# A 64-row product in two PSUM banks in place of a zero-padded one, the output gate made one block later, and a seventh weight buffer

## The chip, the cores and the metric

The kernel runs on one core of a Trainium2 chip. The metric is the device time of one execution in microseconds. A core has a matrix engine (TensorE: PE in the profile, PEld its weight loads), VectorE (DVE), ScalarE (ACT), GpSimd (POOL) and a queue engine (SP) that here issues every DMA. SBUF is the on-chip memory of 128 partitions; PSUM, into which TensorE writes, has eight banks of 512 fp32 values per partition.

## What is computed

A decoder block over 2048 positions and 1024 channels, with two mixers side by side; cut from the reference:

```python
mod = jnp.einsum('bd,de->be', jax.nn.silu(c), ada_w[l]) + ada_b[l]
shift, scale, gate = jnp.split(mod, 3, axis=-1)
h = _rmsnorm(x, norm_g[l]) * (1.0 + scale[:, None, :]) + shift[:, None, :]
p = jnp.einsum('bsd,de->bse', h, w_in[l])            # 1024 -> 9344 channels
...
# RWKV-7 mixer, 16 heads of 64, for every position t:
sk = jnp.einsum('bhvk,bhk->bhv', state, kk_t)
state = (state * w_t[:, :, None, :] - sk[..., None] * b_t[:, :, None, :]
         + v_t[..., None] * k_t[:, :, None, :])
out_t = jnp.einsum('bhvk,bhk->bhv', state, r_t)
...
m = jax.nn.sigmoid(g_conv) * y_conv + jax.nn.sigmoid(g_rwkv) * y_rwkv
out = jnp.einsum('bsd,de->bse', m, w_out[l])
x = x + gate[:, None, :] * out
return _rmsnorm(x, final_g)
```

`y_conv` is a causal depthwise convolution of width 31 with a layer norm and gates. The gate of the last-but-one line is one number per channel, made from `c` alone; the kernel multiplies it into the columns of `w_out`.

## The kernel before

**Stages.** The sequence is cut into four blocks of 512 positions (`NB`, `TB`). The first stage (to about 2500 us) runs over the blocks, and in a block over four groups of four heads; the second stage does the output projections of all blocks. Each of the first three blocks also makes the input of the next one (`xnorm`), and the last one begins the second stage's work for block 0.

**Projections.** Every weight tile (128 channels, 1024 x 128, 4 KB per partition) is used as two parts, a rounded high part and the rest, and three products are summed (`mm3k`, L205). In block 0, `load_w` loads the fp32 tile (`w_st`, L185), ScalarE rounds it (L188), VectorE or GpSimd subtracts (L190), and both parts are stored to DRAM (L194, L195); the later blocks load the two parts (L181, L182). All of these share the pool tag "w" with `WB` = 6 buffers.

**A group.** `group` (L575) drives two pairs of heads through `pair` (L457), a generator in three steps, in the order `ORD`; then it inverts small triangular blocks on GpSimd (L627, L629), and runs the state over eight chunks of 64 positions (L677 to L701): a product of the state into an `xo` bank (L686), 64 x 64 products (L691), and the update of the state (L697, L701). A pair holds two heads of 64 channels: head 0 on partitions 0 to 63, head 1 on 64 to 127.

**The A products** (L528 to L541) are the third step of a pair: for each head and each chunk, a 128 x 128 matrix of products between the tiles `BK` and `KR` over the head's 64 channels. The eight chunks go in two quarters of four (`c4`). To keep one head out of the other's product, ScalarE copies the head's 64 rows of `BK` into `BKz` (L531), a tile of 4 KB per partition whose other 64 rows were set to zero once at the start (L287 to L289), and TensorE multiplies over all 128 rows (L537). Each head's four products fill one bank of tag "aux", and VectorE multiplies it with a mask into `As` (L539).

**PSUM.** Eight banks: two "main" for projections, one "late", `PXB` = 2 for "xo" (the scan), one for the convolution, and `PAB` = 2 for "aux", which the steps of `pair` and L599 use in turn. In block 0 the first four projections are made while the input comes in (`hprep0`, L379), and hold the two "main" and the two "xo" banks until they are used.

**The gate.** `silu_row` makes the row silu(c), broadcast over the partitions, in a buffer of tag "KR" (L260). After the first group of block 0 (`GG` = 0) `ada_cols` loads eight rows of the gate's matrix in pieces of 128 x 1024 into buffers of tag "As", multiplies and sums each on VectorE (L225), and the finished gate goes to DRAM as `grow_d` (L911 to L916).

**Stored weights.** The weights of the second stage are made in spare places: `ogate` (L147) loads a half tile of `w_out`, multiplies it with the gate from DRAM (L156), splits it (L157, L158) and stores both parts; `keep` (L164) does the same without a gate for the two other output projections (L170 to L173). Block 1 does the 16 halves of `ogate`, block 2 the 32 halves of `keep`. They use the shared tag "hx" of seven buffers of 2 KB (`HXB`), as do the input norm and others.

**The order of the work** on each engine is laid down when the program is built: the tile framework keeps the dependencies, and a simulated timeline with priorities decides which ready instruction comes next in an engine's queue. On the chip each queue runs in that order. The loops that fill a group with projections (`NEXT`, `FIRST`, `fill`) are written by hand.

Of the kernel before, what the change touches and what calls it, by code (L numbers as in the profile page):

```python
# [9 lines left out]
F32 = mybir.dt.float32  # L10
# [3 lines left out]
ALU = mybir.AluOpType  # L14
# [4 lines left out]
P = 128  # L19
D = 1024  # L20
KT = D // P
TB = 512
NTT = TB // P
CH = 64
NCH = TB // CH
# [6 lines left out]
KRB, TKB, ASB = 4, 3, 4  # L32
# [2 lines left out]
W2 = 4  # L35
HB = 8
HXB = 7
GG = 0
PXB, PAB = 2, 2
VVT, SHT, RKT, RHT, YT = "r", "sh", "k", "sh", "M"  # L40
ORD = (0, 0, 1, 0, 1, 1)
OE, LE, CE = 0, 0, 1
WLL = 1
TRE = 1
MS, MS2 = 2, 1
WB = 6
KEPT = ("in",)
def lplan(t):
    n = {"c": 0, "g": 0}
# [33 lines left out]
def hybrid_block(ctx: ExitStack, tc: tile.TileContext, x, vecs, convk, w2a2, final_g, ada, w_in, w_co, w_ro, w_o, crow, out,  # L83
                 seq=2048, groups=(0, 1, 2, 3), phase2=True, dbg=None):
    nc = tc.nc
# [4 lines left out]
    cst = ctx.enter_context(tc.tile_pool(name="cst", bufs=1))  # L90
    whl = ctx.enter_context(tc.tile_pool(name="whl", bufs=2))
    dp = ctx.enter_context(tc.tile_pool(name="dp", bufs=1, space=DRAM))
# [10 lines left out]
    u_dram = [dp.tile([P, TB], F32, name=f"u_d{j}", tag=f"u_d{j}") for j in range(KT)]  # L103

    grow_d = dp.tile([D], F32, name="grow_d", tag="grow_d")


    ident = cst.tile([P, P], F32, name="ident")
# [6 lines left out]

    g_col = cst.tile([P, KT], F32, name="g_col")
    hgate_col = cst.tile([P, KT], F32, name="hgate_col")
    shift_col = cst.tile([P, KT], F32, name="shift_col")
    ones = cst.tile([P, P], F32, name="ones")
    nc.vector.memset(ones, 1.0 / D)  # L120
# [11 lines left out]
    def flat(ap):  # L132
        return ap.rearrange("p a b -> p (a b)")
# [85 lines left out]
    def ada_cols(srow, pool, tag, bufs, pairs):  # L219

        for rows, dsts in pairs:
            st = pool.tile([P, 2, D], F32, name="ada_st", tag=tag, bufs=bufs)
            for m in range(2):
                nc.sync.dma_start(st[:, m, :], ada[rows[m]])
                nc.vector.scalar_tensor_tensor(out=st[:, m, :], in0=st[:, m, :], scalar=1.0, in1=srow, op0=ALU.mult,  # L225
                                               op1=ALU.mult, accum_out=dsts[m])
            yield
# [19 lines left out]
    pm = ctx.enter_context(tc.tile_pool(name="pm", bufs=2, space=PSUM))  # L247
    c1 = late.enter_context(tc.tile_pool(name="c1", bufs=1))
    l3 = late.enter_context(tc.tile_pool(name="l3", bufs=3))
# [15 lines left out]
    ab = vc("ada_b")  # L265
# [16 lines left out]
    def headsum(ps, full, hi):  # L282
# [1 line left out]
        nc.gpsimd.tensor_tensor(out=lo, in0=full, in1=hi.bitcast(F32), op=ALU.subtract)  # L284
        nc.tensor.matmul(ps, bones, hi, start=True, stop=False)
        nc.tensor.matmul(ps, bones, lo, start=False, stop=True)
    BKz = c1.tile([P, 2, NCH // 4, 4 * CH], F32, name="BKz")  # L287
    nc.gpsimd.memset(BKz[64:128, 0], 0.0)
    nc.gpsimd.memset(BKz[0:64, 1], 0.0)  # L289
    hones = bones.bitcast(F32)[:, 0::64]  # L290
    keepm = c1.tile([P, TB // 2], mybir.dt.bfloat16, name="keepm")
    nc.vector.memset(keepm, 1.0)
# [38 lines left out]
    def hx(name):  # L331
        return xp.tile([P, TB], F32, name=name, tag="hx")
# [44 lines left out]
    front = {}  # L377

    def hprep0(xs, ada_steps):  # L379


        ss = e2.tile([P, 5, NTT], F32, name="ss0", tag="ss0", bufs=1)
        s2, ss, rs, rt = ss[:, 0:2, :], ss[:, 2, :], ss[:, 3, :], ss[:, 4, :]
        for tt in range(NTT):
            for half in range(2):
                nc.scalar.activation(hx("xsq0"), xs[tt][:, half * TB:half * TB + TB], AF.Square,
                                     accum_out=s2[:, half, tt:tt + 1])
        nc.vector.tensor_tensor(out=ss, in0=s2[:, 0, :], in1=s2[:, 1, :], op=ALU.add)
        nc.vector.tensor_scalar(out=ss, in0=ss, scalar1=1.0 / D, scalar2=RMS_EPS, op0=ALU.mult, op1=ALU.add)
        rsqrt(rs, ss, None, nc.vector, rt)  # L390
        dg = e2.tile([P, NTT, P], F32, name="dg", tag="yj", bufs=1)
        for tt in range(NTT):
            nc.vector.tensor_scalar(out=dg[:, tt, :], in0=ident, scalar1=rs[:, tt:tt + 1], scalar2=None, op0=ALU.mult)
        h = ([], [])
        tiles_ = (T_LORA, T_K, T_R, T_V)
        wf_ = {}
        for k in range(KT):
            next(ada_steps)
            pt = (pl, pc)[k % 2].tile([P, NTT, P], F32, name="ps_x", tag=("late", "acc")[k % 2])
            for tt in range(NTT):  # L400
                nc.tensor.matmul(pt[:, tt, :], xs[tt][:, k * P:(k + 1) * P], dg[:, tt, :], start=(tt == 0),
                                 stop=(tt == NTT - 1), skip_group_check=True)
            hf = hx("hf0")
            nc.scalar.activation(hf, flat(pt), AF.Identity, scale=g_col[:, k:k + 1], bias=shift_col[:, k:k + 1])
            hsplit(h, k, hf)
            for i, ti in enumerate(tiles_):
                if k == i // 2:
                    hl = None
                    if i >= 2:
                        hl = [l3.tile([P, KT, P], F32R, name="w_f", tag="tk", bufs=TKB) for _ in range(4 - i)]  # L410
                        if i == 3:
                            hl.append(lt.tile([P, KT, P], F32R, name="w_f", tag="La", bufs=1))
                    wf_[ti] = load_w("in", ti, hl)
                    front[ti] = (pm, px)[i // 2].tile([P, TB], F32, name="ps_f", tag=("main", "xo")[i // 2])

            for i, ti in enumerate(tiles_):
                if ti in wf_ and k > i // 2:
                    for kk in range(0 if k == i // 2 + 1 else k - 1, k):
                        mm3k(front[ti], wf_[ti], h, kk)
        for ti in tiles_:  # L420
            mm3k(front[ti], wf_[ti], h, KT - 1)
        return h
# [34 lines left out]
    def pair(b, q_, pr, h, lora, uv, Asb, rn, res):  # L457
# [68 lines left out]
        yield  # L526

        for c4 in range(NCH // 4):  # L528
            for hh in range(2):
                hs = slice(64 * hh, 64 * hh + 64)  # L530
                nc.scalar.copy(BKz[hs, hh], BK[hs, c4 * 2:c4 * 2 + 2])  # L531
            for hh in range(2):
                pA = pa.tile([P, 2, 256], F32, name="aux", tag="aux")
                for c in range(4):
                    cc, e = (c4 * 4 + c) // 2, c % 2
                    es = slice(e * 128, e * 128 + 128)
                    nc.tensor.matmul(pA[:, c // 2, es], BKz[:, hh, c // 2, es], KR[:, cc, es],  # L537
                                     start=(c == 0), stop=(c == 3), skip_group_check=True)
                nc.vector.tensor_tensor(  # L539
                    out=Asb[:, hh, c4 * 4:c4 * 4 + 4, :].rearrange("p (a e) n -> p a (e n)", e=2),  # L540
                    in0=pA, in1=flat(maskA).unsqueeze(1).broadcast_to([P, 2, 256]), op=ALU.mult)  # L541
        for e in range(2):
            sl = prow(e)
            tri = Asb[sl, :, e::2, kcol(e)]
# [302 lines left out]
    def lora_split(h):  # L847
# [11 lines left out]
            nc.scalar.copy(dst[os_], lx[os_])  # L859
        return lw, la  # L860

    mod = lt.tile([P, 16], F32, name="mod", tag="rn")

    def ada_steps():
# [8 lines left out]

    for b in range(NB):
        h = hprep(b) if b else hprep0(x0, ada_steps())
        lora = lora_split(h)
        for g in groups:
            if b + 1 < NB:
                xnorm(b + 1, XN[g])
            else:  # L880
                z_first(ZN[g])
                if g < 3:
                    lnorm_first(g)
            if b + 1 < NB:
                todo = [(w, 2 * g + m) for w, m in (FIRST if b == 0 and g == 0 else NEXT)]
            else:
                todo = [wj for i in range(g, 4 if g < 3 else 5) if i == g or g == 3 for wj in lplan(LP)[i]]

            if b == 1:
                for _ in range(2):  # L890
                    n_ = later.pop(0)
                    for half in range(2):
                        ogate(n_, half)
            if b == 2:
                for _ in range(4):
                    n_ = pending.pop(0)
                    for half in range(2):
                        keep(*n_, half)

            def fill(step, n=None):  # L900
                for _ in range(n or (FILL0[step] if b == 0 and g == 0 else 0)):
                    w, j = todo.pop(0)
                    if w == "c":
                        conv(b, h, j)
                    else:
                        gates(b, h, j, w)

            wcount[0] = WSH
            group(b, g, h, lora, fill)
            if b == 0 and g == GG:  # L910
                for _ in ada_cols(srow, l3, "As", ASB, [((16 + k, 17 + k), (hgate_col[:, k:k + 1], hgate_col[:, k + 1:k + 2]))  # L911
                                                        for k in range(0, KT, 2)]):
                    pass
                nc.vector.tensor_tensor(out=hgate_col, in0=hgate_col, in1=ab[:, 16:24], op=ALU.add)
                nc.vector.tensor_scalar(out=hgate_col, in0=hgate_col, scalar1=0.5, scalar2=None, op0=ALU.mult)
                nc.sync.dma_start(grow_d.rearrange("(n p) -> p n", p=P), hgate_col)  # L916
            wcount[0] = WDVE
            if todo:
                fill(0, len(todo))
# [239 lines left out]
```

## Time and profile before

| | |
|---|---|
| median of 3 runs | 3060.63 us (3058.7 to 3069.59) |
| the profiled execution | 3065.4 us, span 3063.7 us |
| TensorE busy | 2884.4 us, 94% of the span, mean granted clock 0.975 |
| VectorE, GpSimd, ScalarE busy | 2056.4, 1257.8, 1011.7 us |
| DMA | 697.15 MB, mean 228 GB/s |

The profile is of one execution, so its durations are set against its own 3065.4 us. "Busy" counts the time in which an engine has at least one instruction in flight; a matrix product's record covers its way through the array, so the records of products that follow each other overlap, and the distance of their starts tells what one costs. An fp32 product appears as two records (passes) here, one of the reduced fp32r type as one. In a row of instructions stand the line of the program, the engine, the operation, out<-in, the shapes (for a product first rows*columns of the array that it takes), the count, then busy time, mean ns of one, and the idle time of the engine before them with what ended it. A row of waits reads: engine and line, what it waited for, us in total, times, longest.

### The profile page before, as it was taken

The numbers are of one execution on the slowest core, as the hardware profiler recorded it, in microseconds if no ns is written. First come the engines' busy times: TensorE is split into PE (matmuls) and PEld (weight loads), VectorE is DVE, ScalarE is ACT, GpSimd is POOL, SyncE is SP. The second block draws the span as 40 slices with busy tenths as digits, with TensorE's granted clock in tenths as the row PEclk, the third lists the DMA queues.
The fourth block names the chain that finished last, engine by engine and source line by source line (L and its number), as shares of the span: only waits on it lengthen the run. The fifth ranks groups of instructions, "written<-read, shape, count | busy, mean of one in ns | idle before, by whom it ended". The sixth has DMA issues, their size and how long they took to land.

```text
span 3063.7 us, 64834 instructions
## 1 busy us (share of the span) xinstructions
PE 2884.4 (94%) x25672; PEld 2724.3 (89%) x25672; DVE 2056.4 (67%) x3879; ACT 1011.7 (33%) x1887; POOL 1257.8 (41%) x1788
## 2 busy tenths in 40 slices
PE   6789898999999999999999999999999999899998
PEld 5789897989999999999999999999989878678988
DVE  6677767786767676777677677767598445766333
ACT  4424343434233242424242424132433113333101
POOL 3455554533453435243434446426367016544000
PEclk9989999999999999999999999999999999999999
DMA  8766757674748477548576787546447678978674
GB/s 301 218 234 210 246 197 257 229 235 150 236 153 258 148 243 242 185 156 273 169 262 199 250 290 267 175 153 214 158 154 265 201 273 312 330 281 309 223 275 173
DMA packets 366368, 697.15 MB, mean 228 GB/s; under 512 B 135984, under 2 KB 154736, under 8 KB 366064
## 3 DMA queue, kind: packets, MB, share of 16 engines
q1 hardware_dynamic: 366064, 693.00, 67.2%
q8 instruction: 202, 3.31, 0.4%
q14 instruction: 102, 0.84, 0.1%
HBM read 504.04 MB, written 187.70 MB: 226 GB/s over the span
## 4 chain that ended last, share of the span: by engine, by line
PE 46%; DMA 17%; DVE 14%; POOL 11%; issue 5%; SPq 3%; ACT 3%; POOLq 0%; DVEq 0%; ACTq 0%
PE ps_main L205 31%; DMA w_st<-w_in_t 3%; DVE acc L776 3%; POOL TT L629 3%; POOL itmp L627 3%; PE aux L537 3%; DMA w_gr<-grow_d 2%; DMA La<-dA 2%; DMA w_st<-w_ro_t 2%; PE pout L1081 1%; PE pout L1079 1%; PE pout L1080 1%; PE xo L691 1%; DMA w_lo<-kl_in 1%; PE xo L697 1%
## 5 line engine op out<-in xcount | busy, mean ns | idle before, releaser
L205 PE MATMUL ps_main<-h_hi,w_hi 128*128 128x256 f32 x4608 | 958.6, 286 | 37.0 <-ACT w_hi L188 19.2
L205 PE MATMUL ps_main<-h_hi,w_lo 128*128 128x256 f32 x4608 | 960.9, 286 | 12.0 <-POOL w_lo L190 6.3
L205 PE MATMUL ps_main<-h_lo,w_hi 128*128 128x256 f32 x4608 | 961.1, 286 | 0.0
L205 PEld LDWEIGHTS ps_main<-h_hi,w_hi 128*128 128x128 f32 x4608 | 723.9, 191 | 47.3 <-ACT w_hi L188 26.1
L205 PEld LDWEIGHTS ps_main<-h_hi,w_lo 128*128 128x128 f32 x4608 | 722.2, 191 | 21.4 <-POOL w_lo L190 7.5
L205 PEld LDWEIGHTS ps_main<-h_lo,w_hi 128*128 128x128 f32 x4608 | 723.4, 191 | 5.4 <-issue 0.2
L776 DVE SCALAR_TENSOR_TENSOR acc<-u,ck,acc 128x512 f32<-128x512 f32 x928 | 698.3, 752 | 19.3
L627 POOL TENSOR_TENSOR itmp<-La,TT 128x126 f32<-128x126 f32 (+22 forms) x496 | 180.2, 363 | 138.5 <-DMA La<-dA 103.0
L629 POOL TENSOR_TENSOR TT<-TT,itmp 128x126 f32<-128x126 f32 (+22 forms) x496 | 189.1, 381 | 37.0
L190 POOL TENSOR_TENSOR w_lo<-w_st,w_hi 128x1024 fp32r<-128x1024 f32 x47 | 113.1, 2407 | 124.2 <-ACT w_hi L188 110.0
L683 ACT ACTIVATE Se<-S,pe 128x128 f32<-128x128 f32 x256 | 89.0, 395 | 195.8 <-DVE S L701 190.8
L537 PE MATMUL aux<-KR,BKz 128*128 128x128 f32 x1024 | 139.1, 285 | 12.3 <-ACT BKz L531 6.6
L701 DVE TENSOR_TENSOR S<-xo,Se 64x128 f32<-64x128 f32 x256 | 73.5, 287 | 112.3 <-PE xo L697 104.2
L537 PEld LDWEIGHTS aux<-KR,BKz 128*128 128x128 f32 x1024 | 127.7, 198 | 15.2 <-ACT BKz L531 8.5
L188 ACT CAST w_hi<-w_st 128x1024 fp32r<-128x1024 f32 x71 | 74.3, 1047 | 192.2 <-DMA w_st<-w_in_t 136.2
L693 DVE TENSOR_TENSOR uv<-xo,rn 64x256 f32<-64x256 f32 x128 | 53.8, 420 | 93.5 <-PE xo L691 92.1
L539 DVE TENSOR_TENSOR As<-aux,maskA 128x512 f32<-128x512 f32 x128 | 87.2, 688 | 40.8 <-PE aux L537 40.0
L688 DVE TENSOR_TENSOR XO<-xo,XO 128x256 f32<-128x256 f32 x128 | 53.7, 420 | 90.3 <-PE xo L686 76.2
L560 POOL TENSOR_TENSOR vv<-rk,vv 128x512 f32<-128x512 f32 x32 | 45.4, 1420 | 153.7 <-ACT rk L559 146.8
L788 ACT ACTIVATE th<-ps_main 128x512 f32<-128x512 f32 x64 | 38.1, 596 | 193.1 <-PE ps_main L205 186.5
L756 ACT ACTIVATE th<-ps_main 128x512 f32<-128x512 f32 x64 | 38.1, 596 | 180.1 <-PE ps_main L205 161.4
L531 ACT COPY BKz<-BK 64x512 f32<-64x512 f32 x128 | 79.0, 617 | 49.4 <-PE aux L537 32.1
(301 smaller groups left out, 5450.6 us busy)
## 6 DMA issues: line engine op xcount, KB each, us to landing
w_hi<-kh_in SPq DMA_DIRECT2D x219, 512.0 KB, 4.2
w_lo<-kl_in SPq DMA_DIRECT2D x219, 512.0 KB, 5.4
w_st<-w_in_t SPq DMA_DIRECT2D x73, 512.0 KB, 4.8
kh_in<-w_hi SPq DMA_DIRECT2D x71, 512.0 KB, 2.9
kl_in<-w_lo SPq DMA_DIRECT2D x71, 512.0 KB, 4.5
w_hi<-kh_ro SPq DMA_DIRECT2D x32, 512.0 KB, 5.0
w_lo<-kl_ro SPq DMA_DIRECT2D x32, 512.0 KB, 6.0
w_hi<-kh_co SPq DMA_DIRECT2D x32, 512.0 KB, 3.7
```

Of the source, the lines that this page charges most:

```text
L188: nc.scalar.copy(hi, st)
L190: lo_eng.tensor_tensor(out=lo, in0=st, in1=hi.bitcast(F32), op=ALU.subtract)
L205: nc.tensor.matmul(ps[:, qs], ww[:, k, :], aa[k][:, qs], start=(k == 0 and t == 0 and q == 0), stop=(k == KT - 1 and t == 2 and q == ms - ...
L531: nc.scalar.copy(BKz[hs, hh], BK[hs, c4 * 2:c4 * 2 + 2])
L537: nc.tensor.matmul(pA[:, c // 2, es], BKz[:, hh, c // 2, es], KR[:, cc, es], start=(c == 0), stop=(c == 3), skip_group_check=True)
L539: nc.vector.tensor_tensor(out=Asb[:, hh, c4 * 4:c4 * 4 + 4, :].rearrange("p (a e) n -> p a (e n)", e=2), in0=pA, in1=flat(maskA).unsqueeze ...
L627: nc.gpsimd.tensor_tensor(out=tmp[:, :ni, :nt], in0=La[:, j:j + 1, j + 1:].broadcast_to([P, ni, nt]), in1=TT[:, :ni, j:j + 1].broadcast_to ...
L629: nc.gpsimd.tensor_tensor(out=TT[:, :ni, j + 1:], in0=TT[:, :ni, j + 1:], in1=tmp[:, :ni, :nt], op=ALU.add)
L683: nc.scalar.mul(Se[:, q, :], Sg[:, q, :], R[q]["pe"][:, c:c + 1])
L693: nc.vector.tensor_tensor(out=uv[pr_, c].rearrange("p q (h n) -> p q h n", n=64), in0=xo[pr_, 0:2].rearrange("p q (h n) -> p q h n", n=64) ...
L701: nc.vector.tensor_tensor(out=Sg[hs, :, hs], in0=xo[hs, 2:4, hs], in1=Se[hs, :, hs], op=ALU.add)
L776: nc.vector.scalar_tensor_tensor(out=acc if i + 1 < HALO else yj, in0=u[:, i:i + TB], scalar=ck[:, j, i:i + 1], in1=acc, op0=ALU.mult, op1 ...
```

## The change

Four things are changed together. The A products take the 64 rows of their head from `BK` itself, the two heads in turn for each chunk, into two aux banks that are held at the same time; `BKz`, its zeros and its copies go. "xo" gets one bank and "aux" three, and the fourth early projection of block 0 moves from "xo" to "aux". The gate is made in block 1, a quarter after each group, in halves of 512 channels in hx buffers, from the row silu(c) that is put into DRAM early; so `keep` moves from block 2 to block 1 and `ogate` from block 1 to block 2. The 4 KB of `BKz` become a seventh buffer of tag "w".

```diff
-GG = 0
-PXB, PAB = 2, 2
+PXB, PAB = 1, 3
...
-WB = 6
+WB = 7
...
+    srow_d = dp.tile([D], F32, name="srow_d", tag="srow_d")
...
+    ghalf = cst.tile([P, 2, KT], F32, name="ghalf")
...
-    BKz = c1.tile([P, 2, NCH // 4, 4 * CH], F32, name="BKz")
-    nc.gpsimd.memset(BKz[64:128, 0], 0.0)
-    nc.gpsimd.memset(BKz[0:64, 1], 0.0)
...
-                    front[ti] = (pm, px)[i // 2].tile([P, TB], F32, name="ps_f", tag=("main", "xo")[i // 2])
+                    fp_, ft_ = ((pm, "main"), (pm, "main"), (px, "xo"), (pa, "aux"))[i]
+                    front[ti] = fp_.tile([P, TB], F32, name="ps_f", tag=ft_)
...
         for c4 in range(NCH // 4):
+            pA = [pa.tile([P, 2, 256], F32, name="aux", tag="aux") for _ in range(2)]
+            for c in range(4):
+                cc, e = (c4 * 4 + c) // 2, c % 2
+                es = slice(e * 128, e * 128 + 128)
+                for hh in range(2):
+                    hs = slice(64 * hh, 64 * hh + 64)
+                    nc.tensor.matmul(pA[hh][:, c // 2, es], BK[hs, cc, es], KR[hs, cc, es],
+                                     start=(c == 0), stop=(c == 3), skip_group_check=True)
             for hh in range(2):
-                hs = slice(64 * hh, 64 * hh + 64)
-                nc.scalar.copy(BKz[hs, hh], BK[hs, c4 * 2:c4 * 2 + 2])
-            for hh in range(2):
-                pA = pa.tile([P, 2, 256], F32, name="aux", tag="aux")
-                for c in range(4):
-                    cc, e = (c4 * 4 + c) // 2, c % 2
-                    es = slice(e * 128, e * 128 + 128)
-                    nc.tensor.matmul(pA[:, c // 2, es], BKz[:, hh, c // 2, es], KR[:, cc, es],
-                                     start=(c == 0), stop=(c == 3), skip_group_check=True)
                 nc.vector.tensor_tensor(
                     out=Asb[:, hh, c4 * 4:c4 * 4 + 4, :].rearrange("p (a e) n -> p a (e n)", e=2),
-                    in0=pA, in1=flat(maskA).unsqueeze(1).broadcast_to([P, 2, 256]), op=ALU.mult)
+                    in0=pA[hh], in1=flat(maskA).unsqueeze(1).broadcast_to([P, 2, 256]), op=ALU.mult)
...
+    nc.sync.dma_start(srow_d.unsqueeze(0), srow[0:1])
+
+    def gate_cols(g):
+        for half in range(2):
+            hs = slice(half * TB, half * TB + TB)
+            sr = hx("sr")
+            nc.sync.dma_start(sr, srow_d[hs].unsqueeze(0).broadcast_to([P, TB]))
+            for k in (2 * g, 2 * g + 1):
+                at = hx("gt")
+                nc.sync.dma_start(at, ada[16 + k][:, hs])
+                nc.vector.scalar_tensor_tensor(out=at, in0=at, scalar=1.0, in1=sr, op0=ALU.mult, op1=ALU.mult,
+                                               accum_out=ghalf[:, half, k:k + 1])
+        if g == 3:
+            nc.vector.tensor_tensor(out=hgate_col, in0=ghalf[:, 0], in1=ghalf[:, 1], op=ALU.add)
+            nc.vector.tensor_tensor(out=hgate_col, in0=hgate_col, in1=ab[:, 16:24], op=ALU.add)
+            nc.vector.tensor_scalar(out=hgate_col, in0=hgate_col, scalar1=0.5, scalar2=None, op0=ALU.mult)
+            nc.sync.dma_start(grow_d.rearrange("(n p) -> p n", p=P), hgate_col)
...
-            if b == 1:
+            if b == 2:
                 for _ in range(2):
                     n_ = later.pop(0)
                     for half in range(2):
                         ogate(n_, half)
-            if b == 2:
+            if b == 1:
                 for _ in range(4):
                     n_ = pending.pop(0)
                     for half in range(2):
...
             group(b, g, h, lora, fill)
-            if b == 0 and g == GG:
-                for _ in ada_cols(srow, l3, "As", ASB, [((16 + k, 17 + k), (hgate_col[:, k:k + 1], hgate_col[:, k + 1:k + 2]))
-                                                        for k in range(0, KT, 2)]):
-                    pass
-                nc.vector.tensor_tensor(out=hgate_col, in0=hgate_col, in1=ab[:, 16:24], op=ALU.add)
-                nc.vector.tensor_scalar(out=hgate_col, in0=hgate_col, scalar1=0.5, scalar2=None, op0=ALU.mult)
-                nc.sync.dma_start(grow_d.rearrange("(n p) -> p n", p=P), hgate_col)
+            if b == 1:
+                gate_cols(g)
```

## The prediction

> **What bounds the kernel now.** I read the page first, then the stretches of the span by engine, then the waits of TensorE.
>
> ```profile
> span 3063.7 us, 64834 instructions
> ...
> PE 2884.4 (94%) x25672; PEld 2724.3 (89%) x25672; DVE 2056.4 (67%) x3879; ACT 1011.7 (33%) x1887; POOL 1257.8 (41%) x1788
> ...
> PE   6789898999999999999999999999999999899998
> ```
>
> ```profile
> core 0: us, PE busy (x) PEld busy (x) DVE busy (x) ACT busy (x) POOL busy (x), PEclk, DMA share, GB/s
> ...
> 160.00:765.00 605.00, 565.45 (x5413) 545.71 (x5413) 451.43 (x786) 234.52 (x398) 297.43 (x404) 0.97 0.65 220
> 765.00:1345.00 580.00, 563.56 (x5555) 546.47 (x5556) 404.46 (x782) 195.64 (x377) 233.94 (x389) 0.99 0.64 205
> 1345.00:1930.00 585.00, 568.23 (x5624) 549.97 (x5624) 415.18 (x779) 206.21 (x394) 264.68 (x425) 0.99 0.72 238
> ```
>
> ```profile
> PE ps_main L205 <- ACT w_hi L188: 19.2, 4, 9.7
> ...
> PE aux L537 <- ACT BKz L531: 6.6, 3, 5.6
> PE ps_main L205 <- POOL w_lo L190: 6.3, 6, 1.8
> ...
> PE ps_main L205 <- DMA w_lo<-kl_in: 5.7, 7, 2.7
> ...
> PE pout L1079 <- DMA w_hi<-kh_o: 4.8, 1, 4.8
> ...
> PE aux L537 <- DVE As L539: 4.3, 3, 1.7
> ...
> PE ps_main L205 <- DMA w_hi<-kh_in: 4.0, 3, 1.8
> ```
>
> Blocks 1 and 2 (765 to 1345 and 1345 to 1930 us) are TensorE from end to end: 563.6 of 580 us and 568.2 of 585, while VectorE has 170 us free in each and the DMA engines stand at 0.64 and 0.72. Block 0 is looser, 40 of 605 us idle from 160 us on. A busy TensorE is not yet one at its limit, so I looked at starts of single passes, below; they are back to back. So a microsecond of TensorE work taken out of the first 2500 us is worth nearly a microsecond, and work on the other engines is worth only what it made TensorE wait. The waits of TensorE (total, times, longest) are short, and only two kinds touch the change: weights that came late, and the copies into the padded tile.
>
> **The A products: the pass itself.** Rows of the program's lines, and then three stretches of TensorE's timeline (start, length, count; the starts are what I use).
>
> ```profile
> L537 PE MATMUL aux<-KR,BKz 128*128 128x128 f32 x1024 | 139.1, 285 | 12.3 <-ACT BKz L531 6.6 <-DVE As L539 4.3 <-DVE ss L128 1.2
> ...
> L691 PE MATMUL xo<-XO,As 64*64 64x64 f32 x1024 | 90.4, 226 | 3.9 <-DVE XO L688 2.3 <-DVE As L673 1.6
> ...
> L539 DVE TENSOR_TENSOR As<-aux,maskA 128x512 f32<-128x512 f32 x128 | 87.2, 688 | 40.8 <-PE aux L537 40.0
> ...
> L531 ACT COPY BKz<-BK 64x512 f32<-64x512 f32 x128 | 79.0, 617 | 49.4 <-PE aux L537 32.1 <-POOL BK L518 13.6 <-DVE r L436 2.4
> ...
> L599 PE MATMUL aux<-uv,As 64*64 64x64 f32 x1024 | 36.8, 224 | 1.9 <-ACT tk L571 1.9
> ```
>
> ```profile
> 422.84 0.28 PE L205 MATMUL ps_main<-h_hi,w_lo 128*128 128x256 f32 x1
> 422.95 1.95 PE L537 MATMUL aux<-KR,BKz 128*128 128x128 f32 x16
> 424.65 0.36 PE L205 MATMUL ps_main<-h_hi,w_lo 128*128 128x256 f32 x1
> 424.86 0.40 PE L205 MATMUL ps_main<-h_hi,w_hi 128*128 128x256 f32 x2
> ```
>
> ```profile
> 374.13 0.40 PE L205 MATMUL ps_main<-h_hi,w_lo 128*128 128x256 f32 x2
> 374.37 0.40 PE L205 MATMUL ps_main<-h_hi,w_hi 128*128 128x256 f32 x2
> 374.60 0.28 PE L205 MATMUL ps_main<-h_lo,w_hi 128*128 128x256 f32 x1
> 374.81 0.67 PE L691 MATMUL xo<-XO,As 64*64 64x64 f32 x8
> 375.41 0.39 PE L205 MATMUL ps_main<-h_lo,w_hi 128*128 128x256 f32 x1
> 375.64 0.39 PE L205 MATMUL ps_main<-h_hi,w_lo 128*128 128x256 f32 x2
> ```
>
> ```profile
> 131.54 0.40 PE L205 MATMUL ps_main<-h_hi,w_lo 128*128 128x256 f32 x2
> 131.87 2.08 PE L599 MATMUL aux<-uv,As 64*64 64x64 f32 x64
> 133.88 0.50 PE L205 MATMUL ps_main<-h_hi,w_hi 128*128 128x256 f32 x2
> 134.22 0.40 PE L205 MATMUL ps_main<-h_lo,w_hi 128*128 128x256 f32 x2
> ```
>
> The program issues 512 A products (4 blocks, 4 groups, 2 pairs, 2 quarters, 2 heads, 4 chunks); the trace has two passes for each, 1024. An L205 pass takes (374.60 - 374.13)/4 = 0.1175 us. From 422.84 to 424.86 lie 16 passes of L537 and two of L205: (2.02 - 0.235)/16 = 0.1116 us a pass, 1024 x 0.1116 = 114.3 us now. (The group's 139.1 us counts each burst's tail too, which lies under the next pass.)
>
> After the change a product uses 64 rows, and neighbours in the order lie on opposite halves. The trace has no product on 64 rows and 128 columns; the nearest are 64 x 64. L691 keeps to one quarter of the array within a chunk: first to last start (0.67 - 0.226)/7 = 0.063 us a pass. L599 alternates between two quarters (its inner loop runs over e): (2.08 - 0.224)/63 = 0.0295, less than half. So alternating tiles run two at a time at the pace of one, and I take 0.1116/2 = 0.0558 us: 1024 x 0.0558 = 57.1 us, 57.2 less. The bounds are 0.0295 and 0.1116 us; the first is for half as many columns, so the value in the middle is the scaled one, and the upper one is a rival below. The Trainium skill (TensorE: Matmul & The Clock Gate, Measured speedup vs the span model) has 3.07 times for four row tiles, not 4; at the same share of the ideal, two would give 1.54 times, an estimate by that page of 74 us for the passes and a sum 17 us worse. L599 against L691 shows no such loss here (0.0295 against 0.063).
>
> **The A products: going in and out.** Around the L537 burst nothing is lost: the 1.785 us are 16 times the spacing inside it, (1.95 - 0.285)/15 = 0.111. Around a tiled burst something is. L691: 374.60 to 375.64 less two L205 passes is 0.805 us, and 8 x 0.063 = 0.504, so 0.30 us for one visit. L599: 131.54 to 134.22 less four L205 passes is 2.21 us, and 64 x 0.0295 = 1.89, so 0.32. I take 0.32 us a visit. The Trainium skill (TensorEngine Tiling (Array Packing), Key Properties) says that a change of tiling mode drains TensorE; the trace agrees, 0.30 and 0.32 us; without that rule the sum would be some 24 us better. How many visits? One for each pair of products of a quarter would be 64; one for each of today's eight-pass sets, split by other work, 128. The loop now issues both heads in one, and the x16 row shows two sets running unbroken already, so I take 75: 24 us. Bounds 20.5 and 41.
>
> So this part is 57.1 + 24 - 114.3 = -33.2 us, all in stretches where TensorE is the bound.
>
> **The copies.** The 128 copies of L531 vanish (79 us of ScalarE, which is two thirds idle: nothing by itself). TensorE waited for them three times, 6.6 us; a copy is 0.617, so that much of each wait goes and what was behind it (the tile BK) comes due: -2 us, bounds 0 and -6.6.
>
> **Three banks instead of two, one for the scan.** The two products of a quarter now hold two aux banks together. The second quarter finds one free bank and needs the one that L539 reads first; if TensorE reaches it at once it waits up to two multiplications, 2 x 0.688 us, on 32 pairs: 0 to 45 us, and behind the waiting pass in TensorE's queue stand the projections. Today's waits of that kind are 4.3 us in three places, because other passes are put between. I take +2. The single xo bank costs nothing: the next chunk's first product needs the state that L701 writes, and L701 is also the last reader of the bank.
>
> **The gate, moved from block 0 to block 1.** What the removal is worth stands in one place, first in the chain of waits, then in the timeline:
>
> ```profile
> 132.62 8.34 DMA ada_st<-ada_t
> 141.02 13.16 DMA w_st<-w_in_t
> ```
>
> ```profile
> 154.26 1.04 ACT L188 CAST w_hi<-w_st 128x1024 fp32r<-128x1024 f32 x1 [12.39 <-DMA w_st<-w_in_t]
> ...
> 155.35 0.80 PE L205 MATMUL ps_main<-h_hi,w_hi 128*128 128x256 f32 x2 [9.68 <-ACT w_hi L188]
> ```
>
> ```profile
> L225 DVE SCALAR_TENSOR_TENSOR ada_st<-ada_st,srow 128x1024 f32<-128x1024 f32 x24 | 29.5, 1239 | 8.7 <-DMA ada_st<-ada_t 8.7
> ...
> L171 POOL TENSOR_TENSOR w_lo<-w_st,w_hi 128x512 fp32r<-128x512 f32 x32 | 41.8, 1308 | 89.0 <-ACT w_hi L170 79.9 <-DMA kl_co<-w_lo 5.2 <-DMA kl_ro<-w_lo 3.1
> ```
>
> The gate's rows (4 MB in eight loads) are on their way just before this weight tile is issued; it takes 13.2 us to land, and TensorE stands for 9.68 us. With the loads gone I take the whole stall: -9.7, bounds 0 (another load takes their place) and -9.7. In block 1 it comes back as 16 products of 512 elements, half of L225's 1.24 us each, 10 us of VectorE in 170 free, and 24 loads into the shared seven hx buffers. A load that waits for its buffer holds up all behind it in the one DMA queue, weights included; blocks 1 and 2 idle 16 to 17 us each with 16 and 24 such buffers taken per group for stored weights, so heavier use shows no price. I take +2, bounds 0 and +10. The stores of the projection weights (32 halves, L171's 1.31 us of GpSimd each) and of the gated output weights (16 halves) change places between blocks 2 and 1: both blocks have over 300 us of GpSimd free, 0.
>
> **The seventh weight buffer.** The waits for weights without the stall above are 19.2 - 9.7 + 6.3 + 5.7 + 4.8 + 4.0 = 30.3 us. A half tile more of prefetch can remove none (the chain is load, cast, subtract) or perhaps half: 0 to -15. I take -4.
>
> **Sum.** -33.2 - 2 + 2 - 9.7 + 2 - 4 = -44.9 us. The profiled execution took 3065.4 us, 4.8 over the median of 3060.63, well inside the 3058.7 to 3069.59 shown. Taken from the median: 3016 us.
>
> **Rivals.** First, a wait takes the place of the one removed: each pair's second quarter stands for two multiplications, 32 x 1.4 = 45 us, which gives back the sum: 3061 us, and half of it 3038. For it: VectorE runs 0.75 us convolution steps in its queue, so L539 may come late. Against: 4.3 us of this wait today with fewer banks.
>
> Second, on the other side: the two halves don't overlap. All overlapping pairs of the trace write different partitions of PSUM; the new ones write the same 128, in two banks. Then a pass stays at 0.1116 and each visit's 0.32 us is pure loss: with 75 visits +24 - 11.7 (the other terms) = +12, 3073; with 100 visits +20, 3081. It is slower by over 0.5% (15.3 us, about what a measurement of this kernel can tell from no change) from (15.3 + 11.7)/0.32 = 84 visits on. Against it: L599's halves do overlap with separate rows. The break-even pass for the whole change is (114.3 + 11.7 - 24)/1024 = 0.0996 us, so an overlap of a tenth is enough not to lose.
>
> **How the numbers follow.** Forecast 0.78, first rival 0.12, second 0.10. The forecast's good end has 64 visits (-3.5), no aux wait (-2), no price in block 1 (-2), -6.6 for the copies (-4.6) and -15 for the buffer (-11): 2993 us. Its bad end has 128 visits (+17), +10 for the banks, +10 in block 1, the stall half back, nothing for copies and buffer: 44 worse, 3060, where it meets the first rival. The range 2993 to 3055 leaves out the second rival and the dear half of the first. Faster by over 0.5% (below 3045): 0.76 of the forecast and 0.03 of the first rival, 0.79. Slower (over 3076): 0.07 of the second rival and 0.01 of the first, 0.08. Same: 0.13.
>
> **What would show it.** Right: 1024 passes of the A products as 64*128, their bursts of 16 taking about 16 x 0.0558 + 0.32 = 1.2 us between L205 passes; no copies; no stall of 9.7 us near 145 us; TensorE's idle time in block 1 still about 17 us. Wrong: 0.11 us between starts inside a burst (second rival); waits of these products for L539 of tens of us (first rival); bursts cut to four or eight passes; or a shorter TensorE and the same span, with waits for weights or for the scan in its place.

## The result and the profile after

The changed kernel takes 3032.72 us (median of 5 runs, 3028.86 to 3047.45) beside 3064.1 for the kernel before on the same chip: a ratio of 0.9917, 95% interval 0.9895 to 0.9939, 0.8% faster. The forecast was 3016, with 2993 to 3055 as its range; the gain, 25 us by the ratio, is just over half of the 44.9 us worked out, and its parts have other sizes than the prediction gave them. The profiled execution took 3047.45 us, the slowest of its five, so totals below are set against its own span.

From the page, the span, the engines and TensorE's slices; then the same stretches as before:

```profile
span 3045.7 us, 64763 instructions
...
PE 2914.9 (96%) x25672; PEld 2735.9 (90%) x25672; DVE 2058.4 (68%) x3896; ACT 935.2 (31%) x1759; POOL 1250.1 (41%) x1786
...
PE   6999998999999999899999999999999999899998
```

```profile
160.00:765.00 605.00, 574.22 (x5391) 546.59 (x5391) 446.09 (x783) 215.70 (x366) 297.45 (x421) 0.96 0.64 218
765.00:1345.00 580.00, 551.92 (x5344) 529.46 (x5340) 410.21 (x795) 182.03 (x356) 217.94 (x348) 0.98 0.71 226
1345.00:1930.00 585.00, 577.13 (x5579) 554.22 (x5578) 413.86 (x774) 176.44 (x343) 259.19 (x422) 0.98 0.67 216
```

TensorE is busy for longer than before (2914.9 us against 2884.4) in a shorter span. Its work was to shrink by some 33 us; instead the whole gain lies in the time in which it is idle, 130.8 us of the span after and 179.3 before. The prediction's sign that its idle time in block 1 stays at about 17 us did not come true: it is 28.1 us, while that of block 2 fell from 16.8 to 7.9. ScalarE's 79 us of copies are gone, as they should. The rows that answer to the ones shown of before, first TensorE's waits, then two groups of instructions:

```profile
PE xo L684 <- DVE S L699: 14.9, 12, 2.4
...
PE ps_main L206 <- POOL w_lo L191: 5.0, 6, 1.4
...
PE aux L534 <- POOL BK L517: 4.1, 1, 4.1
...
PE ps_main L206 <- DMA w_lo<-kl_in: 3.5, 3, 2.5
...
PE ps_main L206 <- ACT w_hi L189: 3.4, 2, 2.3
```

```profile
L206 PEld LDWEIGHTS ps_main<-h_hi,w_hi 128*128 128x128 f32 x4608 | 735.3, 194 | 24.1 <-ACT w_hi L189 3.9
...
L534 PE MATMUL aux<-KR,BK 64*128 64x128 f32 x1024 | 121.5, 307 | 7.4 <-POOL BK L517 4.1
```

The first of these groups in the kernel before:

```profile
L205 PEld LDWEIGHTS ps_main<-h_hi,w_hi 128*128 128x128 f32 x4608 | 723.9, 191 | 47.3 <-ACT w_hi L188 26.1
```

The wait for rounded weights fell from 19.2 us to 3.4, and the 9.7 us stall is not there. But the products, now 64*128, are busy for 121.5 us where they were for 139.1, not for half. And the weight loads of the projections, which the change does not touch, have grown from 191 to 194 ns in the mean. These two rows are what the experiments had to explain.

The bursts of the products, on TensorE's timeline in one pair of block 2 (first fence), and the passes of the 24 that are in flight between 1477.3 and 1477.8 us (second) and between 1478.1 and 1478.6 us (third):

```profile
1476.89 2.05 PE L534 MATMUL aux<-KR,BK 64*128 64x128 f32 x24
...
1480.72 0.40 PE L206 MATMUL ps_main<-h_hi,w_hi 128*128 128x256 f32 x2
1481.05 1.16 PE L534 MATMUL aux<-KR,BK 64*128 64x128 f32 x8
1482.14 0.50 PE L206 MATMUL ps_main<-h_lo,w_hi 128*128 128x256 f32 x2
1482.48 0.40 PE L206 MATMUL ps_main<-h_hi,w_lo 128*128 128x256 f32 x2
```

```profile
1477.10 0.95 PE L534 MATMUL aux<-KR,BK 64*128 64x128 f32 x14
```

```profile
1477.88 0.94 PE L534 MATMUL aux<-KR,BK 64*128 64x128 f32 x7
```

One pair's 32 passes stand as 24 and 8. In the first part of the 24 (second fence) 14 passes start within 0.7 us, 0.05 us each: the distances alternate between 0.007 and 0.105 us, two passes for one. That is the overlap that the prediction counted on, at its full size. In the last part (third fence) 7 passes take 0.94 us with the tail of the last, 0.11 each: nothing overlaps. The 8 that follow don't overlap either: from 1480.72 to 1482.48 less four projection passes of 0.1197 is 1.28 us, which is 8 x 0.112 and 0.385 for going in and out. So the first quarter alternates between the heads and the second does not. That fits the banks: of three, the first quarter holds two, so the second head of the second quarter had none yet, and the planner that orders the queue put the first head's four products in one row and the second head's later, as a visit of its own. In TensorE's queue 241 of the 429 neighbouring products alternate, 188 lie on the same half, in 83 visits.

### The profile page after: what moved, and what is told of

Its sections match the earlier page's. It is cut to its first block, busy times and chain, and to the rows that moved or that the text cites. A ratio compares the mean times of both kernels' runs of the same rounds, so it can differ in the third digit from the quotient of the medians.

```text
span 3045.7 us, 64763 instructions
## 1 busy us (share of the span) xinstructions
PE 2914.9 (96%) x25672; PEld 2735.9 (90%) x25672; DVE 2058.4 (68%) x3896; ACT 935.2 (31%) x1759; POOL 1250.1 (41%) x1786
## 4 chain that ended last, share of the span: by engine, by line
PE 61%; DMA 16%; DVE 9%; POOL 7%; SPq 3%; issue 2%; ACT 2%; ACTq 0%; DVEq 0%; POOLq 0%
PE ps_main L206 43%; DMA w_st<-w_in_t 3%; PE aux L534 2%; POOL TT L627 2%; POOL itmp L625 2%; DMA w_st<-w_ro_t 2%; DMA w_st<-w_co_t 2%; PE pout L1091 2%; PE pout L1092 2%; PE pout L1090 2%; PE xo L689 2%; DVE acc L774 1%; DMA w_gr<-grow_d 1%; PE xo L684 1%; PE xo L695 1%
## 5 line engine op out<-in xcount | busy, mean ns | idle before, releaser
L206 PE MATMUL ps_main<-h_hi,w_hi 128*128 128x256 f32 x4608 | 971.3, 289 | 12.2 <-ACT w_hi L189 3.4
L206 PE MATMUL ps_main<-h_lo,w_hi 128*128 128x256 f32 x4608 | 971.3, 289 | 0.0
L206 PEld LDWEIGHTS ps_main<-h_hi,w_hi 128*128 128x128 f32 x4608 | 735.3, 194 | 24.1 <-ACT w_hi L189 3.9
L206 PEld LDWEIGHTS ps_main<-h_lo,w_hi 128*128 128x128 f32 x4608 | 733.9, 194 | 8.1 <-issue 0.5
L534 PE MATMUL aux<-KR,BK 64*128 64x128 f32 x1024 | 121.5, 307 | 7.4 <-POOL BK L517 4.1
L534 PEld LDWEIGHTS aux<-KR,BK 64*128 64x128 f32 x1024 | 104.2, 208 | 18.7 <-POOL BK L517 4.3
L562 POOL TENSOR_TENSOR BK<-BK,pe 128x1024 f32<-128x1024 f32 x32 | 62.0, 1939 | 140.7 <-PE aux L534 113.1
L684 PE MATMUL xo<-S,KR 128*128 128x128 f32 x512 | 83.0, 285 | 15.0 <-DVE S L699 14.9
L786 ACT ACTIVATE th<-ps_main 128x512 f32<-128x512 f32 x64 | 38.1, 596 | 190.1 <-PE ps_main L206 168.9
L431 ACT ACTIVATE t<-ps_main,mu 128x512 f32<-128x512 f32 x96 | 65.6, 683 | 97.4 <-PE ps_main L206 90.4
```

Of the source, the lines that this page charges most:

```text
L206: nc.tensor.matmul(ps[:, qs], ww[:, k, :], aa[k][:, qs], start=(k == 0 and t == 0 and q == 0), stop=(k == KT - 1 and t == 2 and q == ms - ...
L431: nc.scalar.activation(t1, ps, AF.Identity, scale=mu1[:, mi:mi + 1])
L534: nc.tensor.matmul(pA[hh][:, c // 2, es], BK[hs, cc, es], KR[hs, cc, es], start=(c == 0), stop=(c == 3), skip_group_check=True)
L684: nc.tensor.matmul(xo[:, q, :], R[q]["KR"][:, cc, es], Sg[:, q, :], start=(q == 0), stop=(q == 1), skip_group_check=True)
```

## The experiments

Theory at the outset: the products gained nothing (busy less, but with 83 visits and half the overlap), and the gain came with the gate's stall. Rivals: the products with their copies; the seventh buffer. Each kernel was timed over five rounds against the kernel before on the same chip.

**e1, the products alone.** The kernel before with the loop of the change, `PXB, PAB = 1, 3`, the fourth early projection in "aux", no `BKz`; gate, storing steps and `WB = 6` as before.

> The kernel before with the 64-row products in two banks and the bank counts 1 and 3 alone: gate in block 0, storing steps where they were, six weight buffers. Theory (the products gained nothing, because in the order of TensorE only 250 of 430 neighbouring products alternate between the halves, and the waits that went with the gate made the gain): within 8 us of the kernel before, with a stall of some 9 us still there between 120 and 160 us. Rival (the products and the vanished copies made the gain): 20 to 30 us faster than before.

3043.62 us, ratio 0.9949 (0.9931 to 0.9968): 15.6 us faster. The theory falls: this part of the change does gain, if half of what was forecast. But the gain is not TensorE's work: in the profiled executions TensorE is busy for 2880.5 us, 3.9 less than before, and idle for 164.6, 14.7 less.

**e2, the gate alone.** The gate's part of the change in the kernel before; in the cut, the first step that changes places is `ogate`, the second `keep`.

```diff
-            if b == 1:
+            if b == 2:
...
-            if b == 2:
+            if b == 1:
...
+            if b == 1:
+                gate_cols(g)
```

> The kernel before with the gate moved to block 1 and the two storing steps exchanged, nothing else: zero-padded products, two and two banks, six weight buffers. Theory: most of the change's gain, 15 to 30 us faster than before. Rival (products): at most 10 us faster, the size of the one stall.

3062.24 us, ratio 1.0004 (0.9988 to 1.0019): nothing. It falls for the gate too. Yet TensorE's longest wait between 100 and 160 us is 2.4 us in this run, the stall is gone; something takes the gain back.

**e3, the change with six weight buffers.**

```diff
-WB = 7
+WB = 6
```

> The changed kernel with six weight buffers in place of seven. If the seventh buffer is worth what the prediction took, 4 us slower than the changed kernel; if the shorter waits for weights in the changed kernel are its doing, 10 to 20 us slower; if it does nothing, within 5 us.

3055.55 us, ratio 0.9982 (0.9966 to 0.9998), against 0.9917 with seven: 20 us for the buffer, five times what I took. TensorE's waits in this run, for the rounded weights and for stored ones:

```profile
PE ps_main L206 <- DMA w_hi<-kh_in: 19.1, 2, 15.6
PE ps_main L206 <- ACT w_hi L189: 18.0, 6, 8.3
```

With seven they are 2.5 and 3.4 us.

**What took the gate's gain: the place of the weights.** In the traces of after, e2 and e3 the distance between the starts of neighbouring projection passes (those under 0.13 us, some 12,400) is 119.7 ns in the mean; before it is 117.5 and in e1 117.4. What all three have, and the other two lack, is the gate's code. That code brings a 64-byte tile, `ghalf`, in the pool of constants, which lies ahead of the weight buffers: they begin at byte 2944 of a partition before (128 modulo 256), at 3008 after (192 modulo 256).

**e5, 64 unused bytes ahead of the weights, in the kernel before.**

```diff
+    pad64 = cst.tile([P, 16], F32, name="pad64")
+    nc.vector.memset(pad64, 0.0)
     shift_col = cst.tile([P, KT], F32, name="shift_col")
```

> The kernel before with one unused tile of 64 bytes per partition in the pool of constants, ahead of the weight buffers: same instructions in the same order (one memset more), every later tile 64 bytes further, the weight buffers at 64 modulo 128 bytes as in the changed kernel, and not at 0. Theory (the gate's new small tile moved the weights, and that alone makes a projection's pass 119.7 ns and not 117.4): passes at 119.7 ns, 13,800 x 2.2 ns = 30 us slower than before. Rival (the gate's work or its DMAs slow the passes): 117.4 ns and no slower.

**e6, the same bytes behind the weights**, in the pool `c1`.

> The same 64 bytes behind the weight buffers: weights at 0 modulo 128 as before, all tiles of the pools after them 64 bytes further. If the place of the weights is the cause, 117.4 ns and no slower than before (within 5 us). If it is another tile's place (KR, BK, As, the sums' constants), 119.7 ns and 30 us slower.

e5: 3067.94 us, ratio 1.0030 (1.0019 to 1.0041), 9 us slower, with passes at 119.7 ns. e6: 3058.03 us, ratio 1.0000 (0.9989 to 1.0010), 117.4 ns. The groups of e5 and then of e6, of which the mean duration (after the comma) of a weight load is the number to see:

```profile
L207 PEld LDWEIGHTS ps_main<-h_hi,w_hi 128*128 128x128 f32 x4608 | 736.8, 194 | 45.4 <-ACT w_hi L190 27.6 <-DVE carry L440 4.4 <-DVE th L760 2.8
```

```profile
L205 PEld LDWEIGHTS ps_main<-h_hi,w_hi 128*128 128x128 f32 x4608 | 724.2, 191 | 44.1 <-ACT w_hi L188 24.7 <-DVE carry L440 3.8 <-DVE u L771 2.6
```

So the place of the weight buffers sets the pass, and the gate's tile moved them. The size was off: some 28 us more of passes made the kernel 9 us slower, not 30.

**e7, the change with 64 bytes more, and e12, the kernel before with 128**: both put the weights at byte 3072, 0 modulo 512.

> The changed kernel with 64 unused bytes more ahead of the weight buffers, so that the weights are at 0 modulo 128 again. Theory: passes back at 117.4 ns and some 30 us faster than the changed kernel, about 3002 us where that one has 3033. Rival (not the address): no faster.

> The kernel before with 128 unused bytes ahead of the weight buffers: weights at 0 modulo 512 as in the aligned changed kernel. The passes of the projections should take 115.0 ns and not 117.4, 30 us less TensorE work. If TensorE's time is the kernel's time, 25 to 30 us faster; if only a third comes through, as with the 64 bytes (29 us more of passes, 10 us more of time), 10 us faster.

e7: 3006.75 us, ratio 0.9833 (0.9813 to 0.9853), passes at 115.0 ns; against the change's 0.9917 that is 26 us. e12: 3048.3 us, ratio 0.9966 (0.9953 to 0.9979), 114.5 ns: 10 us faster for 36 us less of passes (12,400 x 2.9 ns), where e7 has 26 us for 58 (12,400 x 4.7 ns). The passes became faster than those of the kernel before, not only as fast, and between a quarter and half of that became time. e7 is faster than both kernels.

**e4 and e8, alternation in both quarters**, e4 on the change, e8 on e7.

```diff
+            prev = None
...
-                    nc.tensor.matmul(pA[hh][:, c // 2, es], BK[hs, cc, es], KR[hs, cc, es],
-                                     start=(c == 0), stop=(c == 3), skip_group_check=True)
+                    with tc.issue_after(prev) if prev is not None else ExitStack():
+                        prev = nc.tensor.matmul(pA[hh][:, c // 2, es], BK[hs, cc, es], KR[hs, cc, es],
+                                                start=(c == 0), stop=(c == 3), skip_group_check=True)
+                    prev = prev.ins if hasattr(prev, "ins") else prev
```

> The changed kernel with each A product tied behind the one before it in TensorE's order, so that the heads alternate in both quarters (419 neighbours alternate and none follows on the same half, in 93 unbroken runs, against 241 and 188 in 83). Theory (an overlapped pass costs 0.056 us, one that isn't 0.112): some 180 more products overlap, 0.11 us each, so 20 us less TensorE work, minus waits for the second bank: 5 to 20 us faster than the changed kernel. Rival (row halves do not gain from overlap, or the wait for the mask multiplication takes it back): no faster, and up to 30 us slower.

> The changed kernel with both: the weights at 0 modulo 128, and the A products tied so that the heads alternate in both quarters. If the alternation is worth something by itself, 5 to 20 us faster than the aligned one; if the run with the alternation alone (3038.5, no faster than the changed kernel) holds, the same as the aligned one within 6 us.

e4: 3038.5 us, ratio 0.9934 (0.9914 to 0.9954), the change's own to within the intervals. e8: 3014.92 us, ratio 0.9858 (0.9842 to 0.9874), 8 us slower than e7 if anything. The products did what the forecast said of them. Their group in e7, then in e8:

```profile
L536 PE MATMUL aux<-KR,BK 64*128 64x128 f32 x1024 | 118.3, 302 | 7.1 <-POOL KR L524 4.0 <-POOL BK L519 2.2 <-ACT ta L475 0.9
```

```profile
L538 PE MATMUL aux<-KR,BK 64*128 64x128 f32 x1024 | 95.0, 303 | 4.2 <-POOL KR L524 2.6 <-POOL BK L519 1.1 <-DVE As L542 0.4
```

And the first 2500 us of e7, then of e8:

```profile
0.00:2500.00 2500.00, 2372.03 (x22869) 2255.79 (x22870) 1785.26 (x3319) 800.28 (x1472) 1097.29 (x1678) 0.97 0.67 223
```

```profile
0.00:2500.00 2500.00, 2344.60 (x22872) 2226.37 (x22873) 1784.67 (x3318) 801.54 (x1472) 1096.65 (x1678) 0.98 0.67 223
```

23 us less of products, and TensorE idle for 27 us more in the same stretch with the same number of passes. The waits of e8 that grew stand in many places:

```profile
PE late L744 <- POOL XO L739: 14.8, 7, 3.4
PE ps_main L208 <- DMA w_lo<-kl_in: 14.5, 2, 13.2
```

In e7 these were 8.7 and 3.0 us. The wait for the mask multiplication, which the first rival feared, is not among them: TensorE waited 0.4 us for it at the products of e8.

**e9, the bank counts alone, and e10, the products with one head after the other** (no copies, same banks, 62 neighbours alternating and 362 not).

> The kernel before with the bank counts 1 and 3 and the early projection moved alone: zero-padded products and their copies stay. Theory (the gain of the products alone, 15 us, is theirs and that of the vanished copies): within 5 us of before. Rival (the third aux bank made that gain): 10 to 15 us faster. If the single bank of the scan costs something, slower than before, with longer waits of the scan's first product for the state.

> As e1, the 64-row products alone, but with one head's four products after the other's in the program, so that almost no neighbours are on opposite halves (62 alternate and 362 do not). No copies, the same banks. If the overlap made e1's gain, no faster than before, since the visits to the tiled mode stay and a pass is at 0.112 us. If the vanished copies made it, as fast as e1, 10 to 15 us faster than before.

e9: 3066.66 us, ratio 1.0028 (1.0015 to 1.0041), 9 us slower. e10: 3071.84 us, ratio 1.0051 (1.0032 to 1.0070), 16 us slower. By the ratios e10 is 31 us behind e1. Yet e10 does not take the overlap away. The products' group in e1, then in e10, and a row of e10 in whose queue eight passes of head 0, eight of head 1 and eight of head 0 follow each other:

```profile
L533 PE MATMUL aux<-KR,BK 64*128 64x128 f32 x1024 | 112.4, 291 | 5.9 <-POOL TT L619 2.2 <-ACT ta L472 2.0 <-POOL BK L516 1.2
```

```profile
L533 PE MATMUL aux<-KR,BK 64*128 64x128 f32 x1024 | 123.5, 297 | 3.8 <-ACT ta L472 1.6 <-POOL BK L516 1.2 <-DVE As L536 0.6
```

```profile
861.07 2.26 PE L533 MATMUL aux<-KR,BK 64*128 64x128 f32 x24
```

From the first to the last start of that row lie 1.99 us, where 24 passes one after the other would take 2.68 (0.213 for the first distance, as in the rows of eight, and 22 of 0.112): from the fifth pass on, most start in pairs 0.004 to 0.006 us apart, so the next head's passes begin ahead of their turn, beside the last ones of the head before. In the whole run 181 such pairs overlap (starts less than 0.06 us apart), 254 in e1 and 448 in e8. So e10 has less overlap, not none, and of the 24.1 us between the spans of the two profiled executions (3069.2 and 3045.1) the products' group explains 11; the projection passes explain 10 more, as more of them ran at half the clock (mean granted clock 0.971 against 0.975). What the kernel would take without any overlap is not shown. That e10 is slower than before fits the price of the visits: 88 of them at 0.385 us are 34 us, the pairs save 181 x 0.112 = 20, and TensorE is busy for 2899.4 us where it was for 2884.4. What makes e9 slower is open: the wait for the scan's state is no longer than before (4.9 us against 5.3), but the order of all queues is planned anew, and TensorE waits 28.8 us for rounded weights where it was 19.2 (e5, with the banks of before, has 26.0).

**e11, the products and the buffer, the gate left in block 0.**

> e1 with the seventh weight buffer: products and buffer, the gate left in block 0, the weights at 128 modulo 256 bytes as in the kernel before. If the buffer is worth the 20 us that it is in the changed kernel, 20 us faster than e1, about 35 faster than before, that is faster than the changed kernel, and TensorE waits for the rounding of weights in block 0 under 10 us where e1 has 28.9. If not, as e1.

3026.2 us, ratio 0.9904 (0.9885 to 0.9922): 14 us less than e1. The wait for rounded weights in e1, then in e11:

```profile
PE ps_main L205 <- ACT w_hi L188: 28.9, 6, 7.5
```

```profile
PE ps_main L205 <- ACT w_hi L188: 9.7, 5, 2.6
```

Without the gate's part the change is as fast as with it, to within the intervals.

## Why the prediction was right in time, and wrong in its parts

By ratios against before: products and banks -0.51%, buffer on top of them -0.45%, gate 0.0%; together -0.9%, and -0.83% was measured. In microseconds, term by term:

- **The products, -33.2 forecast, -15.6 measured (e1, with the banks and without the copies).** The step that failed is "I take 0.1116/2 = 0.0558 us", for all 1024 passes. The rate was right, the share was not: half of them overlap. I had seen that the second quarter finds one free bank, and priced it as a wait of TensorE. But the order of the queue avoids that wait: TensorE is hardly ever idle for a bank there, while in most pairs the second quarter runs head after head and costs a visit more. The visits were 83 for 75 taken, 0.385 us each for 0.32. With these sizes nothing is left of the term: in e1 254 pairs save 28 us and 82 visits cost 32, and TensorE's busy time fell by 3.9 us, not by 33. So the 15.6 us are not the gain that was worked out, but shorter waits of TensorE (164.6 us idle in place of 179.3); at the products themselves it idles 5.9 us where it was 12.3, and where the rest comes from is not shown. The banks with the moved projection, in a plan of their own, cost 9 us (e9), where I had argued nothing for the single xo bank; which part it is, no run separates. On the overlap, the Trainium skill (TensorE: Matmul & The Clock Gate, Measured speedup vs the span model) would have led to 1.54 times for two tiles, an estimate from its figure for four. The trace has two passes in 0.007 + 0.105 us, the full 2 times of 0.112, so the rows were the better guide.
- **The copies, -2 forecast.** Not measured by itself. The 6.6 us of waits for them are gone in e1.
- **The gate, -7.7 forecast, +1 measured (e2).** The stall went as forecast: against e5, the kernel before with its weights at the same place, e2 is 0.26% or 8 us faster (1.0004 and 1.0030, two intervals that just touch). What I missed is in the diff's least line, a 64-byte tile in a pool that lies ahead of the weights: 9 us (e5).
- **The seventh buffer, -4 forecast, -14 (e11 against e1) and -20 (the change against e3) measured.** I let it remove a small part of the waits for weights; it removed two thirds of those in block 0 and a 15.6 us wait for a stored tile. The bound of 15 that I gave was too near for the second of these.
- **That a microsecond of TensorE work "is worth nearly a microsecond"** is the step under all the terms, and it failed. Three runs changed the pace of TensorE's passes alone: +28 us of passes made +9 (e5), -36 made -10 (e12), -58 made -26 (from the change to e7). A fourth changed the order of the products too, and its 23 us less of them made nothing or a loss (e7 to e8). A small part of what is missing is the granted clock. Its mean over the runs was 0.9762 in e5 and 0.9734 in e12, beside 0.9750 and 0.9755 of the kernel before on the same chips: by these shares of 3057 us, an estimate, e5 was some 4 us shorter and e12 some 6 us longer for it. That TensorE is busy for 97% of blocks 1 and 2 does not say that it sets their length: its queue is a fixed order, and in the rows of waits stand the scan and the weights with gaps of mostly 1 to 4 us, which may come due as soon as TensorE gets there sooner. Which of them sets the end in place of TensorE is not settled here: the waits that grew in e8 are spread over several.

The second rival, a loss because the halves don't overlap, did not come about: they do. But its price is real: in e10, with less overlap, the visits cost more than the pairs save. The first, a wait in place of the one removed, is what met the other half of the alternation (e8), at other places than the one it named. That the total fell in the range is in part luck: a product term too large and a buffer term too small offset each other, and the time came out of TensorE's waits, not out of its work.

## What to carry to other kernels

Before a gain is counted for each instance of a loop, see whether the buffers let every instance run in that form: this planner did not wait for a bank, it broke the form up. A new tile, however small, moves all that is allocated behind it; compare the mean duration of instructions that the change does not touch, and put small tiles last. And the price of a microsecond on a busy engine is best measured: pad, shift or double something on it alone. Where a change was to save an engine's work, compare its busy time before and after, and not the kernel's time alone.

## What the runs showed of the hardware that was not expected

The start address of fp32r weights in SBUF sets the pace of a product with 256 columns: 114.5 to 115.0 ns between starts with the buffers at byte 3072 (0 modulo 512), 117.4 at 2944 (128 modulo 256) and 119.7 at 3008 (192 modulo 256), with the tiles of `h`, the moving operand of 13,824 of the 15,360 passes, at the same address in all. The mean weight load was 191, 191 and 194 ns. Where the granted clock was half, the distance was 229 to 230 ns at all three places. Shown is the dependence on the place of the weights (e5 against e6); why it is so was not tried. Two row halves that write the same 128 partitions, in two banks, do run at once (0.007 us between their starts), which no row of before had shown. And where the queue of e10 has eight passes of one half and then eight of the other, pairs begin with the fifth pass: by that order, the second half's passes start ahead of their turn.
